# Seven Strassen-Winograd products of a weight pair summed in two PSUM banks, with the pair's end put off behind the next pair's start

## The chip, the cores and the metric

The kernel runs on one core of a Trainium2 chip. The metric is the device time of one execution of the whole program, in microseconds (us). A core has five engines that matter here: TensorE (PE in the profile; PEld is its weight load), VectorE (DVE), ScalarE (ACT), GpSimd (POOL) and SyncE (SP), which issues the DMAs between the core's memory (SBUF) and the chip's. TensorE writes its results to PSUM; VectorE and ScalarE read them from there.

## The reference, cut to what matters

One layer of an encoder on 1024 tokens of 1024 channels, in float32:

```
x = LN1(a*x + 0.5*SwiGLU_1(x))                    # FFN 1, inner width 2816
x = LN2(a*x + W_o[RMS(FoX(x)) || RMS(ShortConv(x))])   # the mixer
x = LN3(a*x + 0.5*SwiGLU_2(x))                    # FFN 2
x = LN4(a*x + sigmoid(x W_g + b_g) * (p W_p))     # gated embedding

SwiGLU(x) = (silu(x W_gate) * (x W_up)) W_out
proj = x @ w_mix_in                # [q | k | v | forget | B | C | h], 512 columns each, forget 8
FoX: softmax attention of 8 heads, logits + c[t] - c[s], c = cumsum(log_sigmoid(forget + b))
ShortConv: B * conv3(C * h)        # causal, per channel, three taps
```

The change concerns the products x W of a wide W: the input products of both FFNs and that of the mixer.

## The kernel before, in words

**Numbers.** Every float32 operand is split into a high and a low part (`put`, L119 to 121: ScalarE casts the high part, L120, VectorE subtracts it for the low one, L121). A product term is then three matmuls, high by high, low by high and high by low (`mm3`, L137 to 140). TensorE's unit here is a matmul of a 128x128 weight piece with 512 tokens.

**x W.** `pair` (L280) takes two 128-column tiles of W that are 1024 rows deep and computes their products with all 1024 tokens by Strassen's scheme in Winograd's form: seven products in place of eight, named after their token operand: A11, A12, S2, S3, S1, A22, S4. Each (`product`, L234) runs over 512 rows of W in four blocks k, 12 matmuls. A11 and A12 need token half 0 alone. `part1` computes these two: A11's sum is copied out of PSUM by ScalarE as s1 (L244), and A12 plus s1 is the first of four results. `combos` makes the four weight sums t1 to t4 on GpSimd (L134). `part2` (L256) computes S2, S3, S1, A22 and S4; the Winograd sums between the products are made on VectorE, each as one addition of a PSUM bank and an earlier sum (`plus`, L258): u2 = S2 + s1, u3 = S3 + u2, S1 + u3 (a result), u4 = S1 + u2, A22 + u3 and S4 + u4 (results).

**Early pairs.** While the token operands of half 1 (S1, S2, S3, A22, S4) are still being made (`turn1`, L174), `ahead` runs `part1` for some pairs, and s1 waits in DRAM (`s1_d`); `pair` with a number n loads it again (a buffer of `raw`). There are six early pairs in each FFN and eight in the mixer; the full ones are 16, 16 and 4. The stretches in which half 1's operands are made are called the fills.

**Who takes the results.** A pair hands each result to a sink. In `ffn_in` (L292) the gate's sink writes the sum to SBUF and ScalarE applies silu (L303); the up sink writes its sum, GpSimd multiplies it with the silu (L311), and SyncE stores h (L312). In the mixer, `ch_sink` forms C * h, L626 to 628 are the convolution on VectorE, `b_sink` (L601) multiplies by B (L606), collects squares and splits the result; `v_sink` and `qk_sink` (L510) prepare the attention's operands. `sums` (L477) has TensorE add the collected squares up (L484, L485), put off by two products (`later`, `flush`). `forget` (L540) computes the forget gates of a token half; the second call stands behind the second pair (L623).

**Stores and their turn.** PSUM is one pool of eight banks of 128x512; each product takes the next free bank. Weight loads have six buffers (`raw`), split weights seven high and seven low (`wh`, `wl`), weight sums five (`tmp`), Winograd sums `u` six in the FFN and five in the mixer. The order of the instructions on each engine is not that of the code: a scheduler sets it, which simulates the program and places an instruction when its operands and a buffer are there. `ffn_out` multiplies h by W_out by Strassen's scheme on another cut and reloads h from DRAM; attention and the last product follow. Their code is not touched.

## Time and profile before

| | us |
|---|---|
| device time, median of 3 runs | 2026.71 |
| lowest and highest of them | 2024.58, 2034.36 |
| span of the profiled execution | 2030.0 |

The span is that of one execution taken by the hardware profiler. The program runs in this order: FFN 1's input product to about 446 us, its output product to about 716, the mixer's input product to about 947, attention and the mixer's output to about 1266, FFN 2's input product to about 1660, its output to about 1905, the embedding to the end. Four kinds of views are used below: the page's head (span, busy share of each engine), windows (busy time and instruction count of each engine in a stretch, with TensorE's granted clock, 1.00 being the higher of its two levels), waits (the idle time of an engine by what ended it), and timelines with the start and length of single instructions. A matmul's listed length overlaps with the next one's; its pace is the distance between starts.

### The profile page before, as it was taken

What the parts mean: (1) busy time and instruction counts of PE and PEld (TensorE: products, weight loads), DVE (VectorE), ACT (ScalarE), POOL (GpSimd) and SP (SyncE); (2) the same over time, 40 slices, a digit from 0 to 9 for tenths busy, and PEclk for the clock granted to TensorE, in tenths of its full rate; (3) what the DMA queues carried; (4) which work ended last, traced back from release to release, by engine and by line L of the source; (5) the groups of instructions that cost most, each with busy time, mean ns of one, the idle gap of its engine ahead of it and who ended that gap; (6) DMA issues with size and microseconds to landing.
All of it is one profiled execution on the core that took longest, in us unless ns stands there. A gap on an engine that the chain in (4) does not pass through costs nothing.

```text
span 2030.0 us, 25555 instructions
## 1 busy us (share of the span) xinstructions
PE 1905.7 (94%) x8624; PEld 1546.0 (76%) x8624; DVE 1532.3 (75%) x2164; ACT 798.6 (39%) x1422; POOL 951.2 (47%) x669
## 2 busy tenths in 40 slices
PE   8899999999999989798899999999999998889986
PEld 6688888888777767686688787788888886667765
DVE  6975545558999899956888878864544559999978
ACT  5333333335444453233665625433233333333531
POOL 3564443441534265324731324564444447673593
PEclk9999999999999989898999999999999999999988
DMA  6332222268644523378854123332222276653522
GB/s 218 115 130 73 89 89 73 88 241 292 201 153 171 198 89 106 120 257 240 263 149 98 53 99 109 100 124 79 87 84 79 87 265 210 197 188 122 186 67 99
DMA packets 156404, 288.70 MB, mean 142 GB/s; under 512 B 17216, under 2 KB 25664, under 8 KB 156272
## 3 DMA queue, kind: packets, MB, share of 16 engines
q1 hardware_dynamic: 156272, 287.06, 42.8%
q8 instruction: 68, 1.11, 0.2%
q14 instruction: 64, 0.52, 0.1%
HBM read 225.06 MB, written 61.93 MB: 141 GB/s over the span
## 4 chain that ended last, share of the span: by engine, by line
PE 30%; DVE 12%; issue 5%; DMA 5%; POOL 4%; ACT 2%; SPq 0%; DVEq 0%; POOLq 0%; ACTq 0%
PE ps L138 8%; PE ps L139 8%; PE ps L140 8%; DVE wl L121 4%; POOL tmp L134 2%; DMA v_d<-sph 1%; DVE tmp L134 1%; PE pt L756 1%; DMA raw<-in_f_out 1%; PE pt L138 1%; PE pt L139 1%; PE pt L140 1%; DVE pr L718 1%; DMA H<-h_d 1%; POOL r L962 1%
## 5 line engine op out<-in xcount | busy, mean ns | idle before, releaser
L134 POOL TENSOR_TENSOR tmp<-raw 128x512 f32<-128x512 f32 x222 | 346.5, 1562 | 442.7 <-DVE wl L121 216.5
L120 ACT CAST wh<-tmp 128x512 fp32r<-128x512 f32 x444 | 267.2, 620 | 496.4 <-PE ps L139 252.1
L121 DVE TENSOR_TENSOR wl<-tmp,wh 128x512 fp32r<-128x512 f32 x444 | 401.3, 917 | 54.6 <-ACT wh L120 54.1
L139 PE MATMUL ps<-S,wh 128*128 128x512 f32 x896 | 353.8, 395 | 10.7 <-DVE S L121 10.7
L138 PE MATMUL ps<-S,wh 128*128 128x512 f32 x896 | 352.5, 396 | 9.3 <-ACT S L120 7.4
L140 PE MATMUL ps<-S,wl 128*128 128x512 f32 x896 | 351.3, 393 | 1.1 <-DVE wl L121 1.1
L139 PE MATMUL ps<-wl,wh 128*128 128x512 f32 x616 | 248.9, 404 | 31.2 <-DVE wl L121 30.7
L120 ACT CAST wh<-raw 128x512 fp32r<-128x512 f32 x239 | 147.1, 622 | 277.6 <-PE ps L139 211.1
L134 POOL TENSOR_TENSOR tmp<-raw,tmp 128x512 f32<-128x512 f32 x112 | 165.8, 1480 | 180.7 <-DVE wl L121 92.2
L121 DVE TENSOR_TENSOR wl<-raw,wh 128x512 fp32r<-128x512 f32 x231 | 186.5, 812 | 79.7 <-ACT wh L120 78.8
L140 PE MATMUL ps<-wh,wl 128*128 128x512 f32 x616 | 243.0, 395 | 0.0
L138 PE MATMUL ps<-wh 128*128 128x512 f32 x616 | 210.2, 394 | 0.0
L139 PEld LDWEIGHTS ps<-S,wh 128*128 128x128 f32 x896 | 170.1, 190 | 50.7 <-DVE S L121 16.1
L138 PEld LDWEIGHTS ps<-S,wh 128*128 128x128 f32 x896 | 170.3, 190 | 50.0 <-ACT S L120 12.0
L140 PEld LDWEIGHTS ps<-S,wl 128*128 128x128 f32 x896 | 170.2, 190 | 38.1 <-DVE wl L121 3.0
L311 POOL TENSOR_TENSOR c<-c,sil 128x512 f32<-128x512 f32 x88 | 140.7, 1602 | 78.8 <-DVE c L246 45.0
L139 PEld LDWEIGHTS ps<-wl,wh 128*128 128x128 f32 x616 | 117.0, 190 | 74.1 <-DVE wl L121 50.7
L138 PEld LDWEIGHTS ps<-wh 128*128 128x128 f32 x616 | 116.5, 190 | 25.0
L140 PEld LDWEIGHTS ps<-wh,wl 128*128 128x128 f32 x616 | 117.4, 191 | 23.2
L258 DVE TENSOR_TENSOR u<-ps,u 128x512 f32<-128x512 f32 x136 | 91.7, 681 | 43.6 <-PE ps L140 43.4
L134 DVE TENSOR_TENSOR tmp<-H 128x512 f32<-128x512 f32 x110 | 104.3, 955 | 1.0
L138 PE MATMUL ps<-A11h,wh 128*128 128x512 f32 x224 | 89.2, 398 | 6.0 <-ACT wh L120 5.8
(281 smaller groups left out, 3671.3 us busy)
## 6 DMA issues: line engine op xcount, KB each, us to landing
raw<-in_f_out SPq DMA_DIRECT2D x264, 256.0 KB, 3.3
raw<-in_f_in SPq DMA_DIRECT2D x200, 256.0 KB, 2.8
h_d<-c SPq DMA_DIRECT2D x88, 256.0 KB, 2.1
H<-h_d SPq DMA_DIRECT2D x88, 256.0 KB, 5.4
z_d<-r SPq DMA_DIRECT2D x16, 512.0 KB, 3.4
raw<-in_w_conv_in SPq DMA_DIRECT2D x32, 256.0 KB, 2.9
raw<-in_w_qk SPq DMA_DIRECT2D x24, 256.0 KB, 4.7
s_d<-s SPq DMA_DIRECT2D x20, 256.0 KB, 2.0
```

Of the source, the lines that this page charges most:

```text
L120: nc.scalar.copy(h, src)
L121: (eng or nc.vector).tensor_tensor(l, src, h.bitcast(F32), op=sub)
L134: eng.tensor_tensor(t, a, b, op=op)
L138: mm(ps, a[0], b[0], start=first, stop=False)
L139: mm(ps, a[0], b[1], start=False, stop=False)
L140: mm(ps, a[1], b[0], start=False, stop=last)
L258: nc.vector.tensor_tensor(o, ps, u, op=add)
L311: nc.gpsimd.tensor_tensor(c, c, sil.pop((j, i, hf)), op=mult)
L718: nc.vector.tensor_scalar(pr[:, 0:w], pr[:, 0:w], l, None, op0=mult)
L756: nc.tensor.transpose(pv[:, j, t, :], prs[t][:, tok(2 * jp + j)], ident)
L962: nc.gpsimd.tensor_tensor(o, o, gb3[:, n, :], op=mult)
```

## The change

**Two banks.** A product can go onto a bank that already holds a sum (`onto`). A11, S2, S1 and S4 follow each other in bank `ba`, S3 and A22 in bank `bb`. After A11, S2 and S1 the running sum in `ba` is copied to SBUF by ScalarE (`keep`: s1, u2, u4). The results are A12 + s1, bb + u4 (behind S3 and S1), bb + u2 (behind A22), and `ba` itself behind S4.

**Early pairs.** Their A11 is in DRAM, so `ba` begins with S2, and `rest` (the loaded s1) is added by VectorE at each read: u2, u4 and the last result.

**Sinks.** A sink may be handed a bank in place of a function. ScalarE then reads it for silu, VectorE multiplies it with the silu (in place of GpSimd), and `v_sink` copies it by ScalarE.

**The pair's end.** A22 and S4 of a pair with their results are put off (`tails`) until the next pair's A11 is written (in an early pair: until its s1 is loaded); `end_pair` runs them at the end. The convolution moves into a function `done` that is called behind S4; `forget(1)` stays where it is in the code and so stands ahead of the second pair's A22 and S4.

```
-    def mm3(ps, a, b, first, last):
-        mm(ps, a[0], b[0], start=first, stop=False)
...
+    def mm3(ps, a, b, first, last, onto=False):
+        mm(ps, a[0], b[0], start=first, stop=False, skip_group_check=onto)
...
-    def product(w, n):
-        ps = bank()
+    def product(w, n, onto=None):
+        ps = onto or bank()
         for k in range(4):
-            mm3(ps, (w[0][:, tok(k)], w[1][:, tok(k)]), (X[n][0][k], X[n][1][k]), k == 0, k == 3)
+            mm3(ps, (w[0][:, tok(k)], w[1][:, tok(k)]), (X[n][0][k], X[n][1][k]),
+                k == 0 and onto is None, k == 3, onto is not None)
...
-        u2 = plus(new(), product(split(t2), "S2"), s1)
-        u3 = plus(new(), product(split(t3), "S3"), u2)
-        p5 = product(split(t1), "S1")
-        sink(1, 1, lambda o: plus(o, p5, u3))
-        u4 = plus(new(), p5, u2)
-        p4 = product(split(t4), "A22")
-        sink(0, 1, lambda o: plus(o, p4, u3))
-        p3 = product(split(b22), "S4")
-        sink(1, 0, lambda o: plus(o, p3, u4))
+    def keep(up, ps, u=None):
+        o = up.tile([P, HB], F32, name="u", tag="u")
+        if u is None:
+            nc.scalar.copy(o, ps)
+        else:
+            plus(ps, u)(o)
+        return o
...
+        if n is None:
+            ba = product(split(b11), "A11")
+            s1, rest = keep(up, ba), None
+        else:
+            ba, s1 = None, load(s1_d[n])
+            rest = s1
+        end_pair()
+        if n is None:
+            sink(0, 0, plus(product(split(b21), "A12"), s1))
+        b12, b22 = b2 or low()
+        t1, t2, t3, t4 = ts or combos(b11, b21, b12, b22)
+        ba = product(split(t2), "S2", ba)
+        u2 = keep(up, ba, rest)
+        bb = product(split(t3), "S3")
+        product(split(t1), "S1", ba)
+        u4 = keep(up, ba, rest)
+        sink(1, 1, plus(bb, u4))
+
+        def tail():
+            product(split(t4), "A22", bb)
+            sink(0, 1, plus(bb, u2))
+            product(split(b22), "S4", ba)
+            if rest is None:
+                sink(1, 0, None, ba)
+            else:
+                sink(1, 0, plus(ba, rest))
+            done()
+
+        tails.append(tail)
```

How the order moves, at three places.

**TensorE, FFN 1's fill.** Before, at the last K block of S2 (ps_577 and ps_695 are the S2 banks of the first two pairs; S2_159 and S2_161 are the high and low parts of the operand's second half):

```order
L139 MATMUL ps_614<-S1_169,wh_610 128x512
L140 MATMUL ps_614<-S1_167,wl_611 128x512
L138 MATMUL ps_577<-S2_159,wh_573 128x512
L138 MATMUL ps_695<-S2_159,wh_691 128x512
L138 MATMUL ps_732<-S1_166,wh_728 128x512
L139 MATMUL ps_732<-S1_168,wh_728 128x512
L138 MATMUL ps_656<-S4_175,wh_652 128x512
L139 MATMUL ps_577<-S2_161,wh_573 128x512
L140 MATMUL ps_577<-S2_159,wl_574 128x512
L139 MATMUL ps_695<-S2_161,wh_691 128x512
```

and after, at the same block (ps_576 and ps_689 are now the `ba` banks of the two pairs):

```order
L139 MATMUL ps_576<-S2_159,wh_572 128x512
L139 MATMUL ps_689<-S2_159,wh_685 128x512
L140 MATMUL ps_576<-S2_161,wh_572 128x512
L141 MATMUL ps_576<-S2_159,wl_573 128x512
L140 MATMUL ps_689<-S2_161,wh_685 128x512
L141 MATMUL ps_689<-S2_159,wl_686 128x512
L139 MATMUL ps_576<-S1_166,wh_608 128x512
L140 MATMUL ps_576<-S1_168,wh_608 128x512
L141 MATMUL ps_576<-S1_166,wl_609 128x512
```

Parts of S1, A22 and S4 stood ahead of and between the last block of S2 and now stand behind it; S1 goes into the bank that S2 filled, two matmuls after S2's last one there, and S4 follows S1 in it.

**VectorE, the mixer's fill.** Before, from the low part of S4's last K block on (u_6794 is the first sum of the first pair, L595 forms C * h):

```order
L121 TENSOR_TENSOR S4_6196<-tt_6760,S4_6194 128x512
L121 TENSOR_TENSOR wl_6977<-tmp_6915,wh_6976 128x512
L121 TENSOR_TENSOR wl_6997<-raw_6907,wh_6996 128x512
L258 TENSOR_TENSOR u_6794<-ps_6799,raw_6780 128x512
L121 TENSOR_TENSOR wl_7073<-raw_7056,wh_7072 128x512
L121 TENSOR_TENSOR wl_7092<-raw_7058,wh_7091 128x512
L258 TENSOR_TENSOR u_6813<-ps_6818,u_6794 128x512
L258 TENSOR_TENSOR u_6849<-ps_6836,u_6813 128x512
L258 TENSOR_TENSOR u_6851<-ps_6836,u_6794 128x512
L258 TENSOR_TENSOR u_6870<-ps_6857,u_6813 128x512
```

and after (L584 to L591 are the forget gate's steps; u_6669 and u_6704 are the first pair's two reads of its bank ps_6656):

```order
L121 TENSOR_TENSOR S4_6054<-tt_6618,S4_6052 128x512
L584 SCALAR_TENSOR_TENSOR tmp_6843<-ps_6826,bf_101,tmp_6844 8x512
L252 TENSOR_TENSOR u_6669<-ps_6656,raw_6638 128x512
L121 TENSOR_TENSOR wl_6898<-tmp_6768,wh_6897 128x512
L585 TENSOR_SCALAR tmp_6844<-tmp_6843 8x512
L121 TENSOR_TENSOR wl_6917<-raw_6760,wh_6916 128x512
L586 TENSOR_TENSOR tmp_6844<-tmp_6844,tmp_6843 8x512
L121 TENSOR_TENSOR wl_6940<-raw_6864,wh_6939 128x512
L589 TENSOR_SCALAR tmp_6843<-tmp_6843 8x512
L590 TENSOR_TENSOR tmp_6843<-tmp_6843,tmp_6844 8x512
L252 TENSOR_TENSOR u_6704<-ps_6656,raw_6638 128x512
L591 SCALAR_TENSOR_TENSOR tmp_6844<-ones_96,flast_103,tmp_6843 8x512
```

The forget gate's steps for half 1 now stand between the first pair's first and second sum.

**VectorE, the end of the mixer's input product.** Before (L516 is the low part in `qk_sink`; wl_8935 and wl_8941 are weights of the p product that runs beside the attention):

```order
L258 TENSOR_TENSOR u_8630<-ps_8617,u_8594 128x512
L258 TENSOR_TENSOR u_8638<-ps_8617,u_8575 128x512
L516 SCALAR_TENSOR_TENSOR spl_8633<-u_8630,sph_8632 128x512
L121 TENSOR_TENSOR wl_8935<-raw_8932,wh_8934 128x512
L258 TENSOR_TENSOR u_8657<-ps_8644,u_8594 128x512
L121 TENSOR_TENSOR wl_8941<-raw_8938,wh_8940 128x512
L516 SCALAR_TENSOR_TENSOR spl_8660<-u_8657,sph_8659 128x512
L258 TENSOR_TENSOR u_8682<-ps_8669,u_8638 128x512
L516 SCALAR_TENSOR_TENSOR spl_8685<-u_8682,sph_8684 128x512
```

and after (ps_8376 and ps_8395 are the last pair's two banks; L548 is the same low part):

```order
L548 SCALAR_TENSOR_TENSOR spl_8331<-u_8328,sph_8330 128x512
L121 TENSOR_TENSOR wl_8572<-raw_8569,wh_8571 128x512
L548 SCALAR_TENSOR_TENSOR spl_8355<-u_8352,sph_8354 128x512
L252 TENSOR_TENSOR u_8424<-ps_8376,raw_8310 128x512
L121 TENSOR_TENSOR wl_8727<-raw_8724,wh_8726 128x512
L252 TENSOR_TENSOR u_8426<-ps_8395,u_8424 128x512
L548 SCALAR_TENSOR_TENSOR spl_8429<-u_8426,sph_8428 128x512
L121 TENSOR_TENSOR wl_8733<-raw_8730,wh_8732 128x512
L252 TENSOR_TENSOR u_8450<-ps_8395,u_8389 128x512
L252 TENSOR_TENSOR u_8474<-ps_8376,raw_8310 128x512
```

Both splits of p's weights stood among the last pair's sums before and stand there now; one of them is now ahead of the sum that A22 waits for, u_8426, since A22 goes into the bank ps_8395 that this sum reads.

## Rows read from the trace of the kernel before

**Rows 1.** The page's head: busy time, share of the span, instructions.

```profile
span 2030.0 us, 25555 instructions
...
PE 1905.7 (94%) x8624; PEld 1546.0 (76%) x8624; DVE 1532.3 (75%) x2164; ACT 798.6 (39%) x1422; POOL 951.2 (47%) x669
```

**Rows 2.** Windows: stretch, its length, busy time (instructions) of each engine, granted clock, DMA.

```profile
core 0: us, PE busy (x) PEld busy (x) DVE busy (x) ACT busy (x) POOL busy (x), PEclk, DMA share, GB/s
41.70:79.80 38.10, 28.62 (x95) 18.33 (x94) 32.87 (x40) 14.10 (x24) 17.29 (x11) 0.91 0.25 83
79.80:440.00 360.20, 359.98 (x1587) 297.29 (x1586) 204.00 (x278) 116.50 (x193) 174.53 (x124) 1.00 0.31 102
...
752.30:836.00 83.70, 82.66 (x360) 65.70 (x359) 83.58 (x111) 27.36 (x46) 35.95 (x20) 1.00 0.31 103
836.00:862.00 26.00, 13.13 (x53) 10.45 (x52) 24.10 (x35) 6.79 (x12) 8.12 (x5) 0.74 0.37 127
...
1300.00:1640.00 340.00, 340.00 (x1501) 281.53 (x1501) 185.39 (x261) 108.62 (x179) 165.13 (x117) 1.00 0.29 96
```

**Rows 3.** Waits of TensorE: who waited, for whom; us in total, times, longest.

```profile
PE ps L484 <- ACT sph L120: 12.9, 2, 12.5
...
PE pt L138 <- DVE u L258: 8.4, 1, 8.4
```

**Rows 4.** Durations by line (ns min/median/max, first and last start in us): additions, copies.

```profile
L258 DVE TENSOR_TENSOR u<-ps,u x136: 672/680/693, 79.8 to 1657.1; 128x512 f32<-128x512 f32 x136
...
L244 ACT COPY s<-ps x56: 572/579/588, 11.1 to 1644.1; 128x512 f32<-128x512 f32 x56
```

**Rows 5.** Timeline of FFN 1's steady part: start, length, engine, line; idle time before.

```profile
208.08 0.39 PE L140 MATMUL ps<-S,wl 128*128 128x512 f32 x1
...
209.19 0.69 DVE L258 TENSOR_TENSOR u<-ps,u 128x512 f32<-128x512 f32 x1 [1.43 <-PE ps L140]
```

**Rows 6.** Windows of TensorE alone: stretch, length, busy time (matmuls), granted clock, DMA.

```profile
0.00:76.00 76.00, 60.69 (x224) 0.96 0.53 170
76.00:88.35 12.35, 11.77 (x49) 1.00 0.42 130
0.00:752.30 752.30, 721.59 (x3121) 0.99 0.44 149
0.00:1286.20 1286.20, 1209.60 (x5578) 0.97 0.45 147
```

**Rows 7.** Timeline of TensorE in the mixer, behind its two long waits.

```profile
851.73 0.77 PE L138 MATMUL ps<-S,wh 128*128 128x512 f32 x1
...
856.15 0.41 PE L139 MATMUL ps<-S,wh 128*128 128x512 f32 x1
...
957.00 0.80 PE L138 MATMUL pt<-wh 128*128 128x512 f32 x1 [8.44 <-DVE u L258]
...
962.15 0.27 PE L708 MATMUL ps_s<-KA,QA 128*128 128x256 f32 x1
```

**Rows 8.** The chain of waits at the end of the mixer: start, length, what.

```profile
948.51 6.42 DMA raw<-in_pT
...
955.65 0.69 DVE wl L121
956.35 0.61 DVE u L258
```

**Rows 9.** Timeline of ScalarE: the forget gate's two functions.

```profile
770.92 1.28 ACT L555 ACT_TABLE_LOAD   x1
...
774.16 0.63 ACT L556 ACTIVATE tmp<-tmp 8x512 f32<-8x512 f32 x1
```

**Rows 10.** The page's DMA issues: count, KB each, median us from issue to landing.

```profile
raw<-in_f_in SPq DMA_DIRECT2D x200, 256.0 KB, 2.8
...
H<-h_d SPq DMA_DIRECT2D x88, 256.0 KB, 5.4
```

**Rows 11.** Waits of ScalarE, the largest group.

```profile
ACT wh L120 <- PE ps L139: 465.6, 269, 5.7
```

More of the change, by code (lines that the diff above doesn't have):

```diff
@@ L232, in flush @@
             later.pop(0)[1]()
-    def product(w, n):
-        ps = bank()
+    def product(w, n, onto=None):
+        ps = onto or bank()
         for k in range(4):
-            mm3(ps, (w[0][:, tok(k)], w[1][:, tok(k)]), (X[n][0][k], X[n][1][k]), k == 0, k == 3)
+            mm3(ps, (w[0][:, tok(k)], w[1][:, tok(k)]), (X[n][0][k], X[n][1][k]),
+                k == 0 and onto is None, k == 3, onto is not None)
         flush(2)
         return ps
-    def part1(up, b11, b21, sink):
-        ps = product(split(b11), "A11")
-        s1 = up.tile([P, HB], F32, name="s1", tag="u")
-        nc.scalar.copy(s1, ps)
-        ps = product(split(b21), "A12")
-        sink(0, 0, lambda o, ps=ps: nc.vector.tensor_tensor(o, ps, s1, op=add))
-        return s1
     def combos(b11, b21, b12, b22):
@@ L275, in ahead, with end_pair @@
+    def keep(up, ps, u=None):
[5 more added lines that the diff above has]
+        return o
+    tails = []
+    def end_pair():
+        while tails:
+            tails.pop(0)()
     def ahead(up, w0, n, sink, b1=None):
-        s1 = part1(up, *(b1 or (load(w0[:, half(0)]), load(w0[:, half(1)]))), sink)
+        b11, b21 = b1 or (load(w0[:, half(0)]), load(w0[:, half(1)]))
+        s1 = keep(up, product(split(b11), "A11"))
+        sink(0, 0, plus(product(split(b21), "A12"), s1))
@@ L278, in ahead, with pair @@
         nc.sync.dma_start(s1_d[n], s1)
-    def pair(up, w0, w1, sink, n=None, pre=False):
+    def pair(up, w0, w1, sink, n=None, pre=False, done=lambda: None):
         def low():
             return load(w1[:, half(0)]), load(w1[:, half(1)])
-        b1 = load(w0[:, half(0)]), load(w0[:, half(1)])
+        b11, b21 = load(w0[:, half(0)]), load(w0[:, half(1)])
         b2 = low() if pre else ()
-        ts = combos(*b1, *b2) if pre else None
-        s1 = part1(up, *b1, sink) if n is None else load(s1_d[n])
-        part2(up, s1, *b1, *(b2 or low()), sink, ts)
+        ts = combos(b11, b21, *b2) if pre else None
+        if n is None:
[6 more added lines that the diff above has]
+        if n is None:
+            sink(0, 0, plus(product(split(b21), "A12"), s1))
+        b12, b22 = b2 or low()
[16 more added lines that the diff above has]
+        tails.append(tail)
@@ L509, in qk_sink, with sink @@
     def qk_sink(p):
[L510 to L512 removed]
+        def sink(j, hf, fn, c=None):
+            if c is None:
+                c = up.tile([P, HB], F32, name="u", tag="u")
+                fn(c)
             sc = 0.125 if j == 0 else 1.0
@@ L620, with conv @@
         nc.vector.memset(ucv[:, 0:2], 0.0)
-        pair(up, w_conv_in[4 + i], w_conv_in[8 + i], ch_sink(i, ucv), i)
+        def conv(i=i, ucv=ucv):
+            yc[i] = y = ycp.tile([P, T], F32, name="yc", tag="yc")
+            cw = [col[:, 64 + 3 * i + j:65 + 3 * i + j] for j in range(3)]
+            nc.vector.tensor_scalar(y, ucv[:, 2:T + 2], cw[2], None, op0=mult)
+            nc.vector.scalar_tensor_tensor(y, ucv[:, 1:T + 1], cw[1], y, op0=mult, op1=add)
+            nc.vector.scalar_tensor_tensor(y, ucv[:, 0:T], cw[0], y, op0=mult, op1=add)
+        pair(up, w_conv_in[4 + i], w_conv_in[8 + i], ch_sink(i, ucv), i, done=conv)
         if i == 1:
             forget(1)
-        yc[i] = y = ycp.tile([P, T], F32, name="yc", tag="yc")
-        cw = [col[:, 64 + 3 * i + j:65 + 3 * i + j] for j in range(3)]
-        nc.vector.tensor_scalar(y, ucv[:, 2:T + 2], cw[2], None, op0=mult)
-        nc.vector.scalar_tensor_tensor(y, ucv[:, 1:T + 1], cw[1], y, op0=mult, op1=add)
-        nc.vector.scalar_tensor_tensor(y, ucv[:, 0:T], cw[0], y, op0=mult, op1=add)
         if i % 2 == 1:
@@ L632, in v_sink, with sink @@
     def v_sink(p0):
-        def sink(j, hf, fn):
+        def sink(j, hf, fn, ps=None):
             c = ccp.tile([P, HB], F32, name="cc", tag="cc")
-            fn(c)
+            if ps is None:
+                fn(c)
+            else:
+                nc.scalar.copy(c, ps)
             def spread():
```

51 lines of the change are left out of this document (26 added, 25 removed).

## The prediction

> **What bounds the kernel now.** I read the share of the engines first: TensorE is busy 94% of a span of 2030.0 us [rows 1]. A share over the whole span hides where the rest lies, so next come the stretches [rows 2]. In the steady part of both FFN input products TensorE has no hole: 359.98 of 360.20 us and 340.00 of 340.00, at 340.00 / 1501 = 0.2265 us per matmul, 2.72 us per product of 12. VectorE works 204.00 and 185.39 us there and GpSimd 174.53 and 165.13: work taken from them in these stretches buys nothing. The change can gain only where TensorE waits. In the stages that it touches these are the fills, in which the operands of token half 1 are made (41.7 to 79.8, where TensorE is busy 28.62 of 38.10 us, 723.6 to 752.3 and 1266 to 1286), and the mixer's input product, where VectorE is the bound: 83.58 of 83.70 us, then 24.10 of 26.00. Two single waits of TensorE lie in the mixer: 12.5 us for the sums of squares (L484), and 8.4 us at its end [rows 3].
>
> **What is removed, and where it counts.** A full pair has 7 VectorE additions on PSUM and one ScalarE copy; it keeps 3 additions and has 3 copies. A pair whose first half was done early goes from 6 additions to 5. An addition takes 680 ns, a copy 579 [rows 4]. In the FFN this is hidden by TensorE before and after: 0. In the mixer up to the sums stand four early pairs and two full ones: 4 x 1 + 2 x 4 = 12 additions, 8.2 us of a VectorE queue that ran without a hole. The 16 GpSimd products that leave the FFN are hidden too.
>
> **What is added: handovers.** Before, each of the seven products has its own PSUM bank, and nobody waits for the reader. Now A11, S2, S1, S4 follow each other in one bank and S3, A22 in another, and between two of them the bank must be read. The price of a bare handover: a product's last matmul starts at 208.08 and the reader at 209.19, 1.11 us later [rows 5]; a copy takes 0.58 or an addition 0.69; the next matmul starts 0.04 us after its release (the addition ends at 956.96, the matmul starts at 957.00, [rows 7, 8]); less the 0.23 us of a matmul's own pace: 1.50 to 1.61, I take 1.5. Seven matmuls in between cover it. I went through TensorE's new order: with other products in between nearly everywhere, only 14 handovers have fewer than seven. Three are in each FFN: two in the fill (S2 to S1 after 2 matmuls, 1.0 us; S1 to S4 bare, 1.5), one bare one at the end of the input product, and none in the steady part, 4.0 us. Eight are in the mixer: seven bare ones and one with five matmuls in between (0.3), 10.8 us, where A22 of the first pair adds one of its own, below. The sum of all is 18.8 us.
>
> The Trainium skill, Perfetto Trace Analysis, section Optimizing Tensor Performance, speaks against the change: independent groups should rotate through the PSUM banks, so that the read of one overlaps the next group. The trace agrees for the kernel before (340.00 of 340.00 busy with seven banks a pair). Taken by the letter, each of 36 full pairs would lose four handovers and each of 20 early pairs three, 204 x 1.5 = 306 us; by the order, other pairs' products lie in between, and it is the 18.8 above.
>
> **What is added: less to do in the fills.** While the four K blocks of each operand arrive, TensorE can do the k part of a product only if its bank is free. Before, seven or eight products are open at once; now S2 and S3 of two pairs, since S1 needs S2 finished and read. When the last block of S2 comes, 224, 3121 and 5578 matmuls of the kernel have started [rows 6]; in the new order 188, 3106 and 5568 stand ahead of the same block's first use. The operands' own chain on VectorE has the same steps in the same order, so I let it arrive when it did. The deficits of 36, 15 and 10 matmuls are 8.2, 3.4 and 2.3 us, since from there both run without holes. In FFN 1 the kernel before still loses 12.35 - 49 x 0.2265 = 1.3 us behind that point [rows 6], which the new one makes up; two weight casts now stand ahead of the last block on ScalarE and VectorE, 0.8 us, there and in the mixer.
> - FFN 1's fill: 8.2 - 1.3 + 0.8 + 1.0 + 1.5 = 10.2.
> - FFN 2's fill: 2.3 + 1.0 + 1.5 = 4.8.
> - The mixer's fill: the second half of the forget gate now stands in it. On VectorE its steps lie ahead of the second partial sum of the first pair, and one waits for two ScalarE functions with their table loads, 770.92 to 774.79, 3.9 us [rows 9], which S1 and A12 cover in part: with the queue's own steps I reckon 2.4 left over (0 to 5), and 0.6 for the sum behind it. So 3.4 + 0.8 + 2.4 + 0.6 = 7.2, without the handovers.
>
> **What the mixer gives back.** The sums' wait: VectorE is 8.2 us shorter, and the sums now stand four products after the last of the convolution's, some 7 us with the exposed handovers, against a chain of some 5 us; I leave 1.5 of the 12.5, a gain of 11.0. Behind that wait the granted clock was 0.74 over 836 to 862 [rows 2]: ten matmuls, from 851.73 to 856.15, took 4.42 us instead of 2.27 [rows 7], at the lower of the clock's two levels (1.2 GHz): 2.2 us given back. At the end of the mixer VectorE's last sums stood behind a split that waited for a load of p, issued at 948.51 and 6.42 us under way [rows 8]. In the new order they stand behind the same loads, but a read of both banks has to follow the last product anyway: 2.2 of 8.4 stay, a gain of 6.2. From 957.00 to 962.15 the next 12 matmuls took 5.15 us instead of 2.7: 2.4 back [rows 7]. The one before the end now gates a product as well (A22 of the last pair): 1.0 (0 to 3). Sum: 7.2 + 10.8 + 1.0 - 11.0 - 2.2 - 6.2 - 2.4 = -2.8.
>
> **Two smaller terms.** The first weights-times-h product of the FFN's output now starts right behind the last S2 product, whose operand's space takes the first h tiles; 18 matmuls, 4.1 us, cover most of a load (5.4 us to landing, [rows 10]), but not the cast behind it: 1.5 each, 3.0 (0 to 8). In the early pairs the partial sum from DRAM keeps its load buffer to the pair's end, so of six buffers one more is held while the next pair's weights come (2.8 us each, [rows 10], one after the other): 1.5 each, 3.0 (0 to 12). The FFN's output, attention and the end are written as before: 0.
>
> **Sum.** 10.2 + 4.8 - 2.8 + 1.5 + 1.5 (the bare handovers at the ends of the input products) + 3.0 + 3.0 = +21.2 us on the profiled span of 2030.0. That execution is 3.3 us over the median of 2026.71, what lies around its span included or not, so I add the difference to the median: 2047.9, say **2048**.
>
> **Rivals.** *The mixer's VectorE decides.* The stretch was VectorE's, and if the additions that go free its queue, the exposed handovers there find their reader idle or TensorE late for other reasons, and the forget gate's wait fits under the products. Then the mixer keeps 3.4 + 0.8 of loss and gives back 12.5 + 2.2 + 8.4 + 2.4 = 25.5, net -21.3, and without the two smaller terms: 10.2 + 4.8 + 3.0 - 21.3 = -3.3, 2023. It would be under 2016 if, in addition, the operands of the three fills came 7 us sooner in sum. For it: 107.7 of 109.7 us busy. Against: every addition that stays now gates a product, where seven banks let VectorE lag by seven products. The Trainium skill, Perfetto Trace Analysis, section Optimizing Scalar/DVE Operations, has this rule: if the DVE is saturated, moving work to ScalarE may make sense. The trace agrees that it is saturated here, and only here. *The copies queue up.* ScalarE stands 465.6 us in casts that wait for TensorE to free a weight buffer [rows 11]. If the copy after S1 stands behind such a cast in every full pair, the slack of 2.72 - 1.5 = 1.2 us is used up, and each further microsecond costs 36: at 1 us, 2048 + 36 = 2084. Against: in the order the three casts ahead of that copy need buffers that are freed two products earlier.
>
> **How the numbers follow.** My forecast has 0.60, the copies' queue 0.08: both slower. The mixer's rival has 0.32, of which 0.22 within 0.5% (10 us, about what a measurement of this kernel can tell from no change) and 0.10 faster. For the range, the unknown terms reach from 0 to +5, +8, +12 and +3, which I don't add up; above, 2068 leaves out the copies' queue, and below, 2020 takes in most of the other rival. The forecast's own range is 2037 to 2068.
>
> **What would show it.** Right: some 10 and 5 us more idle or slow TensorE around 42 to 90 and 1266 to 1300 us; waits of TensorE for a u or c tile's read of some 1.5 us, about ten of them in the mixer; the wait at L484 under 3 us; no hole in the steady FFN. Wrong: holes of equal size in every full pair; a fill that ends as early as before; or idle time of TensorE in the FFN's output that has changed by more than 5 us.

## The result, and the profile after

The changed kernel takes 2077.5 us (median of 4 runs, 2073.97 to 2079.02) against 2028.95 for the kernel before (2024.58 to 2034.36): a ratio of 1.0237, 95% interval 1.0216 to 1.0257, 48.5 us slower. The forecast said slower, 2048, with a range to 2068. The sign was right and the size was not.

The page's head of the changed kernel, as [rows 1]:

```profile
span 2072.2 us, 25394 instructions
...
PE 1919.1 (93%) x8624; PEld 1547.7 (75%) x8624; DVE 1451.0 (70%) x2016; ACT 831.4 (40%) x1496; POOL 910.9 (44%) x653
```

The profiled executions differ by 2072.2 - 2030.0 = 42.2 us. The profiled execution of the changed kernel was its fastest (2073.97 us, 3.5 below the median), and the kernel before's lay above its median (its span alone is over the median time); the 6 us between 42.2 and 48.5 come from this and are in no row. VectorE does 1532.3 - 1451.0 = 81.3 us less, as intended, and the kernel is slower.

To see where, I compare the times at which TensorE has started the same number of matmuls. Windows from the start give these counts (stretch, length, busy time (matmuls), granted clock, DMA share, GB/s). Of the changed kernel:

```profile
0.00:153.00 153.00, 130.50 (x500) 0.90 0.41 140
...
0.00:1258.70 1258.70, 1176.46 (x5401) 0.97 0.44 147
0.00:1393.30 1393.30, 1295.72 (x5900) 0.97 0.43 142
```

and of the kernel before, at the same counts:

```profile
0.00:140.10 140.10, 124.21 (x501) 0.98 0.48 155
...
0.00:1238.00 1238.00, 1167.48 (x5401) 0.97 0.46 149
0.00:1359.20 1359.20, 1282.60 (x5901) 0.97 0.45 146
```

The whole table, from such windows, with the forecast's terms beside it:

| stretch, up to matmul | before, us | after, us | lost in it | forecast |
|---|---|---|---|---|
| FFN 1's fill, 500 | 140.1 | 153.0 | +12.9 | +11.7 |
| its steady part, 1700 | 412.1 | 425.0 | 0.0 | 0 |
| end of its input product, 2000 | 480.1 | 496.8 | +3.8 | +3.0 |
| its output product, 3000 | 715.5 | 730.7 | -1.5 | 0 |
| mixer's fill, 3400 | 818.0 | 842.4 | +9.2 | |
| sums of squares, 3600 | 876.1 | 891.4 | -9.1 | mixer: -2.8 |
| mixer's end, 4400 | 1053.1 | 1074.4 | +6.0 | |
| attention, 5400 | 1238.0 | 1258.7 | -0.6 | 0 |
| FFN 2's fill, 5900 | 1359.2 | 1393.3 | +13.4 | +6.3 |
| its steady part, 7100 | 1631.2 | 1665.3 | 0.0 | 0 |
| end of its input product, 7300 | 1676.5 | 1714.9 | +4.3 | +3.0 |
| its output product, 7900 | 1845.7 | 1889.1 | +5.0 | 0 |
| the rest | 2030.0 | 2072.2 | -1.2 | 0 |

The cuts are by count, so the mixer's end holds some 100 us of the attention too. Most losses are where the forecast put them: the fills, the ends of the input products, the mixer. What is gained at the sums of squares, 9.1, only pays for the mixer's fill, 9.2. Nothing is lost in the steady parts, although the banks are handed over there in every pair: TensorE is busy 290.00 of 290.00 us, as in [rows 2] (a window with all engines, columns as there):

```profile
1380.00:1670.00 290.00, 290.00 (x1281) 240.15 (x1280) 123.98 (x164) 104.72 (x182) 119.21 (x89) 1.00 0.26 89
```

Three stretches miss the forecast by much: FFN 2's fill by 7 us, the mixer by 9 and FFN 2's output product by 5. The waits of TensorE, as [rows 3], show the new kind (a read of a shared bank by VectorE, L252, or ScalarE, L258) and the one that went (the sums, now L515: 12.9 before, 1.7 after):

```profile
PE ps L139 <- DVE u L252: 20.6, 13, 4.7
...
PE ps L139 <- ACT u L258: 5.0, 6, 1.0
...
PE pt L139 <- DVE u L252: 2.7, 1, 2.7
...
PE ps L515 <- ACT sph L120: 1.7, 2, 1.3
```

The first three sum to 28.3 us. Of these, 2.7 stand where the kernel before had its 8.4 at the mixer's end, and 0.6 is a copy of an early part; the other 25.0 are handovers, where the forecast had 18.8 and 1.0 for the last pair's A22. The ones that ScalarE reads cost a wait of 1.0 us or less, under the 1.5 reckoned. Of the ones that VectorE reads the longest is 4.7. FFN 2's fill shows why (timeline of TensorE; by the order printed for FFN 1's fill, the first two rows are S2's last matmuls of the first and of the second pair, and S1 of the first pair runs from 1312.69 to 1317.33):

```profile
1307.17 0.39 PE L141 MATMUL ps<-S,wl 128*128 128x512 f32 x1
...
1307.62 0.39 PE L141 MATMUL ps<-S,wl 128*128 128x512 f32 x1
1312.69 0.79 PE L139 MATMUL ps<-S,wh 128*128 128x512 f32 x1 [4.68 <-DVE u L252]
...
1317.10 0.40 PE L140 MATMUL ps<-S,wh 128*128 128x512 f32 x1
1317.33 0.40 PE L141 MATMUL ps<-S,wl 128*128 128x512 f32 x1
1318.51 0.50 PE L139 MATMUL ps<-S,wh 128*128 128x512 f32 x1 [0.78 <-DVE u L252]
```

and VectorE in the same microseconds:

```profile
1309.07 0.69 DVE L121 TENSOR_TENSOR S<-tt,S 128x512 fp32r<-128x512 f32 x1
1309.67 2.36 DVE L121 TENSOR_TENSOR wl<-tmp,wh 128x512 fp32r<-128x512 f32 x2
1311.95 0.68 DVE L252 TENSOR_TENSOR u<-ps,raw 128x512 f32<-128x512 f32 x1
...
1317.76 1.29 DVE L252 TENSOR_TENSOR u<-ps,raw 128x512 f32<-128x512 f32 x2 [4.53 <-PE ps L141]
```

At 1317.76 the reader stood ready: it had been idle for 4.53 us and reads 0.43 us after S1's last matmul starts. S4 then starts 1.18 us behind that matmul, 0.95 more than the pace of 0.23: this is what a bare handover costs when nothing is ahead of the reader. S2's bank is read 4.78 us after its last matmul (1307.17), since VectorE works in its order and has the last operand block and two weight splits to do first. They stood ahead of the same read in the kernel before:

```profile
1287.99 2.39 DVE L121 TENSOR_TENSOR wl<-tmp,wh 128x512 fp32r<-128x512 f32 x2
1290.31 0.68 DVE L258 TENSOR_TENSOR u<-ps,raw 128x512 f32<-128x512 f32 x1
```

There TensorE had other products open and went on without a wait. Here it has nothing else open and stands 4.68 us. Then the granted clock is at its lower level, 0.50: the ten matmuls from 1312.69 to 1317.10 take 4.41 us instead of 2.27 (window of TensorE):

```profile
1312.70:1316.70 4.00, 4.00 (x10) 0.50 0.18 66
```

### The profile page after: what moved, and what is told of

Its sections match the earlier page's. It is cut to its first block, busy times and chain, and to the rows that moved or that the text cites. A ratio compares the mean times of both kernels' runs of the same rounds, so it can differ in the third digit from the quotient of the medians.

```text
span 2072.2 us, 25394 instructions
## 1 busy us (share of the span) xinstructions
PE 1919.1 (93%) x8624; PEld 1547.7 (75%) x8624; DVE 1451.0 (70%) x2016; ACT 831.4 (40%) x1496; POOL 910.9 (44%) x653
## 4 chain that ended last, share of the span: by engine, by line
PE 32%; DVE 16%; issue 6%; POOL 6%; DMA 4%; ACT 2%; SPq 0%; DVEq 0%; POOLq 0%; ACTq 0%
PE ps L139 8%; PE ps L140 8%; PE ps L141 8%; DVE wl L121 6%; POOL tmp L134 2%; DVE tmp L134 2%; PE pt L799 1%; DMA raw<-in_f_in 1%; POOL r L1006 1%; POOL r L1005 1%; PE pt L139 1%; PE pt L140 1%; PE pt L141 1%; DVE tt L134 1%; PE po L807 1%
## 5 line engine op out<-in xcount | busy, mean ns | idle before, releaser
L139 PE MATMUL ps<-S,wh 128*128 128x512 f32 x896 | 361.1, 406 | 45.4 <-DVE u L252 19.7
L140 PE MATMUL ps<-S,wh 128*128 128x512 f32 x896 | 359.0, 401 | 7.8 <-DVE S L121 7.8
L141 PE MATMUL ps<-S,wl 128*128 128x512 f32 x896 | 357.3, 400 | 3.3 <-DVE wl L121 3.0
L121 DVE TENSOR_TENSOR wl<-raw,wh 128x512 fp32r<-128x512 f32 x231 | 194.5, 846 | 161.6 <-ACT wh L120 147.5
L139 PEld LDWEIGHTS ps<-S,wh 128*128 128x128 f32 x896 | 173.1, 194 | 96.0 <-DVE u L252 22.2
L140 PEld LDWEIGHTS ps<-S,wh 128*128 128x128 f32 x896 | 173.6, 194 | 47.6 <-DVE S L121 12.4
L339 POOL TENSOR_TENSOR c<-c,sil 128x512 f32<-128x512 f32 x72 | 101.4, 1411 | 154.8 <-DVE c L252 130.8
L140 PE MATMUL ps<-A11l,wh 128*128 128x512 f32 x224 | 88.1, 394 | 0.8 <-DVE A11l L121 0.8
```

The source lines that it names most:

```text
L121: (eng or nc.vector).tensor_tensor(l, src, h.bitcast(F32), op=sub)
L139: mm(ps, a[0], b[0], start=first, stop=False, skip_group_check=onto)
L140: mm(ps, a[0], b[1], start=False, stop=False, skip_group_check=onto)
L141: mm(ps, a[1], b[0], start=False, stop=last, skip_group_check=onto)
L339: nc.gpsimd.tensor_tensor(c, c, sil.pop((j, i, hf)), op=mult)
```

## Experiments

All kernels start from the changed one. "Before" is the kernel before, run on the same chip beside each. Most edits put this form of a pair, with a bank for each product and the additions of before, ahead of the new one, under a condition (*CONDITION*):

```
+        if CONDITION:
+            s1 = keep(up, product(split(b11), "A11")) if n is None else load(s1_d[n])
+            end_pair()
+            if n is None:
+                sink(0, 0, plus(product(split(b21), "A12"), s1))
+            b12, b22 = b2 or low()
+            t1, t2, t3, t4 = ts or combos(b11, b21, b12, b22)
+            u2 = keep(up, product(split(t2), "S2"), s1)
+            u3 = keep(up, product(split(t3), "S3"), u2)
+            p5 = product(split(t1), "S1")
+            sink(1, 1, plus(p5, u3))
+            u4 = keep(up, p5, u2)
+
+            def end():
+                p4 = product(split(t4), "A22")
+                sink(0, 1, plus(p4, u3))
+                p3 = product(split(b22), "S4")
+                sink(1, 0, plus(p3, u4))
+                done()
+
+            tails.append(end)
+            return
```

| run | two banks in | us | before | ratio (95% interval) |
|---|---|---|---|---|
| e1_early_old | full pairs; early pairs not put off | 2046.38 | 2029.84 | 1.0082 (1.0064 to 1.0100) |
| e2_full_old | early pairs | 2070.87 | 2029.84 | 1.0201 (1.0186 to 1.0216) |
| e3_own_banks | none, all put off | 2027.11 | 2029.84 | 0.9993 (0.9983 to 1.0003) |
| e4_at_once | all, nothing put off | 2088.33 | 2029.84 | 1.0290 (1.0266 to 1.0315) |
| g1_scalar_reads | all, ScalarE reads bank A | 2073.41 | 2030.85 | 1.0219 (1.0198 to 1.0240) |
| g2_fresh_bank | all, S1 of early pairs in a third | 2057.28 | 2030.85 | 1.0132 (1.0112 to 1.0151) |
| b1_mixer_full_new | full pairs of the mixer | 2026.75 | 2030.85 | 0.9981 (0.9972 to 0.9991) |
| m1_ffn_full_new | full pairs of the FFNs | 2040.90 | 2030.85 | 1.0054 (1.0037 to 1.0072) |
| m2_last_pair_old | the same without each FFN's last | 2032.18 | 2029.79 | 1.0007 (0.9996 to 1.0018) |
| f1_forget_behind | all, forget gate as before | 2077.71 | 2029.79 | 1.0228 (1.0201 to 1.0255) |
| c1_late_sums | none, sums later | 2037.59 | 2029.79 | 1.0037 (1.0024 to 1.0050) |
| c2_and_p_split | none, sums later, p on GpSimd | 2036.29 | 2029.79 | 1.0033 (1.0021 to 1.0045) |
| q1_qk_own | all but the mixer's q and k pairs | 2079.45 | 2031.65 | 1.0236 (1.0214 to 1.0259) |
| q2_ffn_early_own | all but the FFNs' early pairs | 2051.00 | 2031.65 | 1.0090 (1.0073 to 1.0107) |
| b2_b_pairs_only | the mixer's two B pairs | 2029.63 | 2031.65 | 0.9986 (0.9975 to 0.9998) |
| e5_early_own | full pairs, all put off | 2040.01 | 2030.12 | 1.0046 (1.0029 to 1.0063) |

### Banks or order, early or full pairs

**e1_early_old** (CONDITION `n is not None`, with `end_pair()` ahead of `return`).

> Early pairs as before (seven banks, six VectorE additions, nothing put off), full pairs in two banks and put off as in the change. Theory E (the loss sits in the early pairs, whose banks VectorE must read before TensorE goes on, in stretches where VectorE has a queue): the three fills and the end of the mixer come back, 13.8 + 13.4 + 9.7 + 5.8 us of the changed kernel's loss; what stays is the ends of the two FFN input products, 3.8 + 4.2, against some 9 to 13 gained at the sums' wait: 2020 to 2035. Theory O (the loss is in the new order, by the put-off ends of pairs): the full pairs keep their put-off end and most of the loss stays: 2055 to 2080.

**e2_full_old** (CONDITION `n is None`, with the same line).

> The other half: early pairs in two banks and put off, full pairs as before (seven banks, seven VectorE additions), their ends put off too. Theory E: the fills and the end of the mixer lose what they lose in the changed kernel, some 42 us, the ends of the FFN input products lose nothing, and the gain at the sums' wait goes partly away: 2065 to 2080. Theory O: the same range, 2060 to 2080, since the ends are put off. A theory that the full pairs' handovers cost much (F): 2035 to 2050.

The text on record is wrong on one point: as run, the full pairs' ends were not put off (`end_pair()` stands ahead of `return` here too), only the early pairs' were.

**e3_own_banks** (CONDITION `True`).

> Every pair with seven banks and the additions of before; only the end of each pair (A22, S4) is put off behind the next pair's A11. Theory E: no bank is handed over, so the fills cost what they cost before: 2020 to 2035 (the sums' wait may shrink by some us, since the sums stand later). Theory O: most of the loss is there, 2055 to 2080.

**e4_at_once** runs the end of a pair at once:

```
         tails.append(tail)
+        end_pair()
```

> The change with two banks in every pair, but nothing put off: A22 and S4 follow S1 at once. Theory E: the early pairs still hand their banks over, 2065 to 2085, and of the gain at the sums' wait some is lost. Theory O: back to the kernel before, 2020 to 2040.

The order alone costs nothing (e3, 2.7 us below before, within its interval), and putting the ends off helps the two-bank form: without it +58.5 against before (e4, 3 us over its range), where the change has +48.5. So theory O falls. The early pairs alone lose nearly everything (e2, +41.0; both theories had that range, only theory F falls by it). e1 came 11 us over its range's top, +16.5, which goes against the part of theory E by which full pairs lose little. **e5_early_own** (CONDITION `n is not None`) then puts the ends of the early pairs off as well:

> Early pairs in seven banks, full pairs in two, and the ends of all pairs put off. If the parts add up (FFN full pairs +10, mixer full pairs -4 against the kernel before): 2033 to 2039, and the put-off end of the early pairs is worth some 10 us beside full pairs in two banks. If the full pairs lose more together than apart: 2042 to 2050, as with early pairs whose end is not put off.

It gave +9.9, between its two ranges (2040.01, 1 us over the first): of e1's loss 16.5 - 9.9 = 6.6 us is that early pairs were not put off. The parts of the change are then, each difference against its own "before": full pairs +9.9; the early pairs of the FFNs 48.5 - 19.3 = 29.2 (change less q2, below); the rest, 9.4, would be the early pairs of the mixer, which no run takes by themselves.

### What makes the early pairs dear

**g1_scalar_reads**: a sum is copied by ScalarE in the early pairs too, and the partial sum added to the copy.

```
         o = up.tile([P, HB], F32, name="u", tag="u")
-        if u is None:
-            nc.scalar.copy(o, ps)
-        else:
-            plus(ps, u)(o)
+        nc.scalar.copy(o, ps)
+        if u is not None:
+            nc.vector.tensor_tensor(o, o, u, op=add)
         return o
```

> The change, but in the early pairs too ScalarE copies the sum out of bank A, and VectorE adds the partial sum from DRAM to the copy afterwards, off the path of the bank. Theory R (a bank is freed late since its reader stands behind VectorE's queue; 4.3 us after the last matmul in FFN 2's fill instead of 1.1): TensorE's waits for a VectorE read, 23.3 us in the changed kernel, fall under 8, the slow clock behind them goes too, 2045 to 2062. Theory N (the fills are long because fewer products are open): the fills stay within 3 us of the changed kernel's, 2068 to 2080.

**g2_fresh_bank**: in the early pairs S1 starts a bank of its own (`new` makes its first matmul overwrite).

```
-    def product(w, n, onto=None):
+    def product(w, n, onto=None, new=False):
...
-                k == 0 and onto is None, k == 3, onto is not None)
+                k == 0 and (onto is None or new), k == 3, onto is not None)
...
-        product(split(t1), "S1", ba)
+        if rest is not None:
+            ba, rest = bank(), u2
+            product(split(t1), "S1", ba, True)
+        else:
+            product(split(t1), "S1", ba)
```

> The change, but in the early pairs S1 begins a bank of its own (its sum starts from u2), so S2 to S1 is no handover and S1 can be under way in the fills; S1 to S4 and S3 to A22 still share. Theory N: both FFN fills come back to within 4 us of before, 20 us less, and the mixer's fill in part: 2045 to 2060. Theory R: the handovers that are left (S1 to S4, S3 to A22) are read by VectorE as before; in the fills the order has no short one left, so 2050 to 2065, with the end of the mixer as slow as in the change.

g1 lowered the waits for VectorE's reads from 23.3 to 5.6 us, as theory R said, and the time by little (+42.6 against +48.5, where theory R wanted 2062 at most). The reads now wait on ScalarE instead. The same handover in FFN 2's fill, ScalarE's timeline of g1:

```profile
1306.97 0.62 ACT L120 CAST S<-tt 128x512 fp32r<-128x512 f32 x1 [3.06 <-DVE tt L134]
1307.50 1.13 ACT L120 CAST wh<-tmp 128x512 fp32r<-128x512 f32 x2
1308.54 0.61 ACT L120 CAST wh<-raw 128x512 fp32r<-128x512 f32 x1
1309.06 0.57 ACT L257 COPY u<-ps 128x512 f32<-128x512 f32 x1
```

and TensorE's, where the wait is 3.21 us in place of 4.68, with the slow clock behind it all the same:

```profile
1309.69 0.50 PE L139 MATMUL ps<-S,wh 128*128 128x512 f32 x1 [3.21 <-ACT u L257]
```

The last operand's cast, which waits for VectorE, and three weight casts stand ahead of the copy there, as an operand block and two splits stood ahead of the addition. So it is not that VectorE reads, but that at the end of a fill each engine that could read has the operands' and the next weights' work queued, just when TensorE has nothing else open. g2 takes the handover from S2 to S1 away, and with it 22 us. Its time lies in both theories' ranges; its trace speaks for theory N, since up to the 500th matmul and from the 5400th to the 5900th it loses 2.9 and 4.5 us, where the change loses 12.9 and 13.4. But g2 also lets S1 start early, so no run separates the wait from the lack of open products; only the traces do, below. The Trainium skill's rule that independent groups should rotate through the banks (Perfetto Trace Analysis, Optimizing Tensor Performance) points the right way for the fills; the steady parts, where a pair shares its banks too, paid nothing (290.00 of 290.00 us busy).

**q2_ffn_early_own** (CONDITION `n is not None and in_ffn`, where `in_ffn` tells the FFNs from the mixer):

> The change, but the six early pairs of each FFN have seven banks and the additions of before, put off; the mixer and all full pairs stay as in the change. If the fills' loss of 13.8 and 13.4 us is all in the shared banks: 2048 to 2054. If part of it is made by what follows, the full pairs or the order: 2056 to 2068.

2051.0, in the first range. In its trace the two fills take 2.6 us less and 2.0 us more than in the kernel before: both come back whole, and nothing of their loss is made by what follows.

### The full pairs of the FFNs

**m1_ffn_full_new** (CONDITION `n is not None or not in_ffn`).

> Seven banks and put-off ends everywhere, but the 32 full pairs of the FFNs in two banks. Theory E: the steady part has no hole, and the only loss is at the two ends of the input products (3.8 and 4.2 us in the changed kernel) and what follows in FFN 2's output (some 2 to 4): 2034 to 2042. If the full pairs' handovers cost nothing: 2025 to 2030.

**m2_last_pair_old** (CONDITION `n is not None or not in_ffn or last`, `last` being the last pair of an input product).

> As the run with two banks in the FFNs' full pairs only (10 us over the kernel before), but the last pair of each FFN input product has seven banks too. If the whole loss of the full pairs sits at the end of the input products (bare S1 to S4, then a wait for the cast behind the first h load): back to 2026 to 2031, with no wait there and FFN 2's output as before. If the steady part or the copies on ScalarE cost something: 2034 to 2042.

+10.0 and +2.4 (m2's time lies between its two ranges and is not to be told from before): of what 32 full pairs lose, two, the last of each input product, lose 7.7. In m2's trace the ends of the input products lose nothing, but FFN 2's output product still loses 3.2 us, where m1's loses 5.5; so the last pair makes only part of that loss. In the changed kernel the end of FFN 2's input product shows the bare handover and then a cast (waits of TensorE from 1665 to 1700):

```profile
PE ps L139 <- ACT wh L120: 2.4, 1, 2.4
PE ps L139 <- ACT u L258: 0.7, 1, 0.7
```

and in FFN 1 ScalarE's timeline tells what that cast waits for, the load of an h tile:

```profile
452.36 0.62 ACT L120 CAST wh<-H 128x512 fp32r<-128x512 f32 x1 [7.95 <-DMA H<-h_d]
```

### The mixer

**b1_mixer_full_new** (CONDITION `n is not None or in_ffn`) and **b2_b_pairs_only** (CONDITION `n is not None or in_ffn or not pre`; the B pairs alone have `pre`).

> Seven banks and put-off ends everywhere, but the four full pairs of the mixer in two banks. Theory E (the early pairs lose, the mixer's full pairs gain because VectorE has 16 additions less in the stretch that it bounds): the wait for the sums of squares falls from 13 us to under 3, nothing else is lost: 2012 to 2021. If the gain needs the FFN's full pairs or the early ones: 2025 to 2032.

> Seven banks and put-off ends everywhere, but the two full pairs that carry B (ahead of the sums of squares) in two banks; the two v pairs have seven. If the 8 additions saved ahead of the sums are what the gain of the four pairs (2026.75 against 2030.85) comes from: 2022 to 2027; if the v pairs carry it: 2027 to 2031.

b1 is 4.1 us faster than before, not the 10 or more that were expected, and it does not stand apart from e3 (0.9981 and 0.9993, intervals that overlap). b2 is 2.0 us faster than its own before, in the range for the v pairs, but it does not stand apart from b1 or e3 either, so which of the pairs carry the gain stays open. The wait for the sums did fall, to 6.6 us in b2 and to 2.2 in b1. TensorE's waits from 770 to 875 us, in e3:

```profile
PE ps L537 <- ACT sph L120: 13.2, 1, 13.2
```

and in b1:

```profile
PE ps L139 <- ACT u L258: 2.9, 3, 1.0
PE ps L540 <- DVE spl L121: 2.2, 1, 2.2
...
```

One wait of 13.2 has become eight that sum to 9.2. **c1_late_sums** (on e3's form) moves the matmuls of the sums without taking work from VectorE, and **c2_and_p_split** takes a split off VectorE's queue at the mixer's end as well:

```
-        h, l = split(acc.pop(hf), side_ring[0])
+        h, l = split(acc.pop(hf))
...
-                later.append([0, sums(hf, msc)])
+                later.append([-5, sums(hf, msc)])
```

```
-                pt = [split(load(pT[k][:, half(hf)])) for k in range(2)]
+                pt = [split(load(pT[k][:, half(hf)]), eng=nc.gpsimd) for k in range(2)]
```

> Seven banks and put-off ends everywhere; the matmuls of the sums of squares stand five products later, and their operands use the weight buffers. If the 13 us wait is only a matter of where TensorE meets the sums (a late but busy VectorE catches up behind them): under 3 us are left, 2012 to 2019. If VectorE's queue is the bound there, the wait goes to the next products: 2022 to 2028.

> As the one before, and the low parts of p are subtracted by GpSimd, so the last sums of the mixer do not stand behind a split that waits for a load of p on VectorE. If that split is the cause of the wait of 8 to 10 us at the mixer's end, 6 to 8 us less than the one before: 2005 to 2013; if ScalarE's cast or the sums themselves are as late: no change.

c1 is 7.8 us slower than before, outside both ranges. Its waits in the same stretch:

```profile
PE ps L139 <- ACT wh L120: 17.6, 2, 13.5
```

The 13 us did not vanish with the sums; they stand at a product's matmul. This is no clean test of whether VectorE's queue is the bound. Only the matmuls of the sums were moved; the cast of their operand (`acc`) waits for VectorE as before, and on ScalarE it stands ahead of the weight cast that TensorE waits for until 845.83:

```profile
844.64 0.62 ACT L120 CAST wh<-acc 128x512 fp32r<-128x512 f32 x1 [0.68 <-DVE acc L528]
845.16 0.61 ACT L120 CAST wh<-raw 128x512 fp32r<-128x512 f32 x1
```

A run with that cast moved too was not made. In c2, 1.3 us faster than c1, the wait of 9.1 us at the mixer's end (`u`, VectorE) fell to 0.6 and came back in the attention's first microseconds as 7.8 us for another operand (waits from 940 to 970):

```profile
PE pt L139 <- ACT tmp L869: 7.8, 1, 7.8
...
PE pt L139 <- DVE u L252: 0.6, 1, 0.6
```

**f1_forget_behind** calls `forget(1)` from the second pair's `done`, behind its convolution; **q1_qk_own** (CONDITION `n is not None and n > 3 and not in_ffn`) gives the q and k pairs their own banks.

> The change, with the forget gate of token half 1 called behind the second pair's end, as in the kernel before. By the prediction's step (the gate's functions delay the first pair's sums in the mixer's fill by 3 us): 2072 to 2076, and TensorE's 2.6 us wait for a VectorE sum 25 us behind the fill goes. If the gate costs nothing there: 2076 to 2080.

> The change, but the four q and k pairs at the mixer's end have seven banks and the additions of before, put off. If their shared banks make the waits there (five reads by VectorE, 13 us of waiting and a slower clock behind it): the mixer's end loses some 6 to 10 us less, 2067 to 2072. If TensorE waits for VectorE there anyway, in one wait at the end as in the kernel before: 2074 to 2080.

Neither moved the time beyond its interval; both times lie in the range for no gain. f1's mixer fill loses no less than the change's (11.6 us against 9.2 in the traces), and the wait of 2.6 us is still there, 2.66, with a step of the convolution ahead of the read on VectorE. In q1 the six waits for VectorE's reads at the mixer's end are two of 2.3 us in sum, and waits of 4.8, 2.5 and 1.9 us at the start of the attention stand in their place. From the 3600th to the 4400th matmul the traces take 177.1 us before, 183.2 in the change, 180.1 in q1, but 178.1 in f1, which leaves those pairs as they are. Whether the shared banks cost anything at the mixer's end, or only decide where TensorE waits, stays open within some 6 us.

## Why the prediction was right or wrong

**Right: the sign, the places and most of what was counted.** The steady parts have no hole. The operands arrive nearly as before: in FFN 2 the last block of S4 is written to 1309.76, against 1288.07 before, 1.0 us later when the 20.7 that the kernel is behind by then are taken off; in FFN 1 it is written 2.1 us sooner, to 75.92 against 77.99. What fewer open products cost shows at the last matmul of S2, the 192nd in FFN 1 and the 5572nd in FFN 2. Windows up to there of the changed kernel and of the kernel before:

```profile
0.00:76.90 76.90, 56.48 (x192) 0.83 0.51 172
...
0.00:1307.70 1307.70, 1217.17 (x5572) 0.97 0.44 145
```

```profile
0.00:66.70 66.70, 52.19 (x192) 0.96 0.59 190
...
0.00:1284.70 1284.70, 1208.10 (x5572) 0.97 0.45 147
```

That is 10.2 us in FFN 1 (forecast 8.2 + 0.8) and 23.0 - 20.7 = 2.3 in FFN 2 (forecast 2.3). The ends of the input products cost 3.8 and 4.3, where 3.0 was forecast for each, but the halves of that sum were off in opposite ways: in FFN 2 TensorE waits 0.7 for the bare handover and 2.4 for the cast behind the h load, and 1.5 was forecast for either. The sums' wait went from 12.9 to 1.7 (forecast: 1.5 left).

**Wrong: the price of a bare handover.** The step "less the 0.23 us of a matmul's own pace: 1.50 to 1.61, I take 1.5" fails twice. First, the row was misread [rows 5]. The matmul of 208.08 is not the last one ahead of the read at 209.19; that one starts at 208.76 (timeline of the kernel before) and by its listed length ends at 209.15, just ahead of the read:

```profile
208.76 0.39 PE L140 MATMUL ps<-S,wl 128*128 128x512 f32 x1
```

So a reader that waits comes 0.43 us after the start, not 1.11, as at 1317.76 above, and the forecast's own sum gives 0.43 + 0.58 + 0.04 - 0.23 = 0.82 with a copy and 0.93 with an addition. (The 1.1 us in g1's expectation is the same misreading.) Second, this one price, from a row where the reader was waiting for the product, was used for every place, also where the reader has a queue. The waits at the handovers are 0.8 us in FFN 1's fill (forecast 2.5) and 1.4 at the two ends (3.0), where the readers came at once, but 6.0 in FFN 2's fill (2.5) and 16.9 in the mixer (11.8). The two errors go opposite ways, and the second is the larger.

In FFN 2's fill the changed kernel is 23.0 us behind at the 5572nd matmul and 31.1 at the 5600th: the two handovers cost 8.1, of which 4.68 + 0.78 = 5.5 are waiting and 4.41 - 2.27 = 2.1 the slow clock behind it. (The rest is mostly that a wait is counted from the end of a matmul's listed length, 0.39, which is over its pace.) Up to the 5900th it falls behind by 3.0 more, with three short waits, two for weight casts and one for a read, 0.48 + 0.50 + 0.56 = 1.5 us. With the 2.3 above that is 8.1 + 3.0 + 2.3 = 13.4, the whole loss of the fill. The slow clock was in no term: the forecast gave clock back where waits vanish and charged none where waits appear. FFN 1 shows it too. There the handover behind the fill was only 0.78, but behind a wait of 2.80 for an operand the granted clock is at its lower level (0.50 from 75.4 to 81.3), and over 68 to 84 us it is 0.68, where the kernel before has 1.00:

```profile
68.00:84.00 16.00, 10.28 (x26) 0.68 0.14 49
```

```profile
68.00:84.00 16.00, 14.85 (x63) 1.00 0.20 67
```

**Wrong: what the mixer gives back.** The step on the mixer's end took 6.2 us of the 8.4 and 2.4 of clock as gained. The last wait did fall to 2.72, close to the 2.2 forecast, but five waits for VectorE's reads now stand ahead of it (timeline of TensorE):

```profile
939.66 0.80 PE L139 MATMUL ps<-S,wh 128*128 128x512 f32 x1 [4.00 <-DVE u L252]
958.54 0.72 PE L139 MATMUL ps<-S,wh 128*128 128x512 f32 x1 [2.51 <-DVE u L252]
...
984.37 0.50 PE L139 MATMUL pt<-wh 128*128 128x512 f32 x1 [2.72 <-DVE u L252]
```

with one of 2.07 and two of 0.9 between: 13.1 us in sum, where one of 8.4 stood. At the first two of them VectorE is not even busy all the time. At the first it stands twice at low parts of q or k that wait for ScalarE, and the read of the bank is behind them in its order; ScalarE in turn waits for stores of v:

```profile
935.08 0.63 ACT L547 ACTIVATE sph<-u 128x512 fp32r<-128x512 f32 x1 [1.88 <-DMA v_d<-sph]
...
935.75 0.69 DVE L548 SCALAR_TENSOR_TENSOR spl<-u,sph 128x512 fp32r<-128x512 f32 x1 [1.78 <-ACT sph L547]
...
938.92 0.68 DVE L252 TENSOR_TENSOR u<-ps,raw 128x512 f32<-128x512 f32 x1
```

At the second the read, at 957.81, stands behind a split for the p product, whose cast waits for a load:

```profile
955.98 0.62 ACT L120 CAST wh<-raw 128x512 fp32r<-128x512 f32 x1 [4.90 <-DMA raw<-in_w_ple]
956.63 1.26 DVE L121 TENSOR_TENSOR wl<-raw,wh 128x512 fp32r<-128x512 f32 x1 [2.91 <-ACT wh L120]
```

For the last pair the order was in the text, and the forecast counted what stands ahead of its A22 (1.0; the wait is 0.9). It had no such term for the pairs before the last, and none for what the instructions ahead of a read wait for themselves. Beside it stands a second error, to count a wait's length as a gain: b1 and c2 each took one long wait in the mixer away, of 13 and 9 us, and gained 4 and 1.

**Wrong: the forget gate.** The 2.4 + 0.6 us for its steps do not show (f1: no change). **Open:** the early pairs' load buffers were given 1.5 us in each FFN; two waits of 1.0 us in sum for weight casts behind FFN 2's fill may be that, and no run tells. **Wrong: FFN 2's output product,** put at 0 because its code is as before, loses 5.0 us. It comes with the full pairs in two banks (m1's trace loses 5.5 there, e2's, where they have seven, 0.5). TensorE waits there for VectorE's weight splits, in the changed kernel (1700 to 1890 us) and in the kernel before (1665 to 1850):

```profile
PE ps L140 <- DVE wl L121: 25.1, 18, 4.3
```

```profile
PE ps L139 <- DVE wl L121: 21.4, 16, 2.3
```

What makes these waits longer is not resolved. Of the rivals, the copies' queue did not come: no hole in the steady parts. The mixer's rival needed 21.3 us less there and got 6.1 more: the VectorE work was saved, and the waits moved. The range failed because its upper end added one unknown at a time, while the handover's price was held at 1.5 and neither the clock behind a new wait nor FFN 2's output had a term.

## What to carry to other kernels

The price of a wait on a shared bank is set by the reader's place in its own queue, so take it from a row of the same stretch, with what stands ahead of the reader and what that in turn waits for; a price read in a steady part holds for the steady part. When you read a delay off a timeline, check that the instruction you count from is the last one ahead of the event. Sharing a bank cost nothing here where other products lay between, and most in a fill, where fewer open products meant less to do and then nothing to do. A long wait behind a busy engine was not a gain of its length here: taken away, it came back in part or nearly whole at later products.

## What the runs showed of the hardware

Long waits of TensorE in the fills had a second price that I had not expected at that size: the lower clock behind them, 2.1 us after the 4.68 us wait in FFN 2's fill, and a granted clock of 0.68 over 16 us around the 2.80 us wait at the end of FFN 1's. With the reader ready, a bank of 128x512 went from one product to the next in 1.18 us, from the start of the last matmul to the start of the next. A VectorE subtraction of 128x512 that takes 0.68 us elsewhere took 1.75 in the first of the two splits at 1309.67, and 1.79 at the same place in the kernel before (the second took 0.68 in both); a GpSimd multiplication of the same size ran during most of it, from 1309.15 to 1310.88, and no run tells whether that is the cause.
